# Hybrid encoder layer on one Trainium2 core: weight loads queued apart from their splits, output-weight steps taken singly, SiLU by tanh, and mixer A's queries transposed half a head earlier

## The chip, the cores and the metric

The kernel runs on one core of a Trainium2 chip. The metric is device time in microseconds of one execution. Three runs of the kernel before gave 913.66, 912.55 and 913.62 us, median 913.62.

Names of the profile: PE is TensorE's matmul stream and PEld its weight loads, DVE is VectorE, ACT is ScalarE, POOL is GpSimd, SP is the queue that issues most DMAs. L61 is line 61 of the kernel.

## The reference

One layer of a bidirectional encoder over 512 tokens and 16 meta tokens, width 2048, float32:

```python
hn = rmsnorm(h, pre_norm_g)
proj = hn @ w_in
qa, ka, va, ga, qb, kb, vb, gb = split(proj)
ya = gqa_axial_mixer(qa, ka, va, ...) * silu(ga)
yb = diff_attn_mixer(qb, kb, vb, ...) * silu(gb)
y = concat([ya, yb]) @ w_out
out = (h + rmsnorm(y, post_norm_g))[n_meta:]
```

Mixer A is attention with 8 query heads of 128 over 2 key heads, with an RMS norm and a rotary turn of queries and keys. Mixer B is differential attention: 8 heads, each with two softmaxes over 64-wide halves and a distance penalty, subtracted from each other. Both have a SiLU gate of their width.

## The kernel before, in words

**Splits.** Every float32 operand of a matmul is cut in two parts, high and low, so that three matmuls (high by high, low by high, high by low) give the precision. A weight block of 128 x 1024 is a *chunk*: SP loads it into a buffer `st` (three of them), ACT copies it to `wh` (L156) and DVE subtracts to get `wl` (L157), three buffers each. `fetch` (L206) hands one chunk to the matmuls and keeps two more ready or in preparation. `dense_T` (L212) projects 128 columns of `w_in` from two chunks, with 16 x 3 matmuls of 512 columns for the real tokens (`REAL`), or twice as many of 264 columns for all tokens (`KEYS`).

**Stages, in order.** The start; mixer B, where for each of 8 heads the gate, values, keys and queries are projected while the head before them attends; mixer A's keys, values and two groups of queries (`queries_A`); the eight gates of mixer A; the output product in four quarters (`product`, tiles `po`), built on sums of weight blocks.

**Attention beside the projections.** A recording layer (`Lanes`) keeps a clock of matmul time. An attention task is a generator that records a few matmuls, then yields a lag from the table `LAG`; `dense_T` polls the tasks after every three matmuls. So PE's order is fixed by the lags, and Tile's scheduler orders the other engines around it. A tile of 128 queries makes scores `sc` on PE (one PSUM buffer for all tiles), which DVE takes out together with the row maximum (L521 in mixer B, L624 in mixer A), ACT makes the exponentials (L529, L627), POOL scales them (L534, L629), DVE turns them in 32 x 32 blocks (L448). After two tiles, half a head, the result goes to DRAM and back regrouped (`turn<-pt`, `pl<-turn`), is split (`ph`, `pl`, L337 and L340) and meets the values on PE (`pv`).

**Mixer A's queries.** At a head's start `attention_A` (L597) transposes its queries on PE (`tr<-ident,qn`), splits them on ACT and DVE into `qh` and `qlA`, yields the lag `qA`, and takes four tiles with the lag `scA` between them. Head 4 waits for the second group of queries.

**Output-weight sums.** `weigh` (L805) makes 32 sums of blocks of `w_out` in DRAM, while mixer B runs: SP copies a block (`ws<-in_w_o` or `ws<-ws`), then POOL issues a DMA that adds another block onto it (L809). A call with n=2 takes two steps in a row, and the second of them issues the addition to the block whose copy was issued just before.

**Gates.** `gate` (L423) and `silu_A` (L583) take the projection from PSUM with DVE (times the row scale `rB`), then ACT applies its Silu. Silu, Exp and Sqrt each bring ACT_TABLE_LOADs into ACT's stream.

Of the kernel before, what the change touches and what calls it, by code (L numbers as in the profile page):

```python
# [10 lines left out]
F32 = mybir.dt.float32  # L11
# [3 lines left out]
ALU = mybir.AluOpType  # L15
# [14 lines left out]


LAG = dict(vals=3.5, bank=2.8, bankA=1.5, bankB=2.5, turnA=1.5, turnB=1.5, pvA=5.0, pvB=6.0, scB=3.0,
           pB=22.0, ss=6.0, qA=2.35, scA=5.1, pA=16.0, rope=10.2, head=3.85, fin=1.35, qn=1.4, norm=4.0, valsA=(10.0, 7.0),
           steps=(3.0, 2.5, 2.0, 2.0), stepsK=(2.5, 2.0, 1.5))

AHEAD = -60
# [70 lines left out]
def kernel(ctx: ExitStack, tc: tile.TileContext, xT, xn, xm, w_s, w_t, w_q, w_o,  # L107
# [31 lines left out]
    def load(out, in_):  # L139

        tc.keep_in_program_order(nc.sync.dma_start(out=out, in_=in_))


    def wload(src, n=1024, dma=nc.sync.dma_start, parts=1):
        st = wp.tile([P, 1024], F32, name="st", tag="st")
        ws = None
        for i in range(parts):
            c = slice(i * n // parts, (i + 1) * n // parts)
            dma(out=st[:, c], in_=src if parts == 1 else src[:, c])
            ws = wsplit(st, c, ws)  # L150
        return ws
# [49 lines left out]
        mm(ps, wl, xh[k][:, n0:n1], start=False, stop=(k == KT - 1))  # L201


    todo, chunks = [], []

    def fetch(ahead=2):  # L206
        while todo and len(chunks) <= ahead:
            src = todo.pop(0)
            chunks.append(src() if callable(src) else wload(src))
        return chunks.pop(0)  # L210

    def dense_T(segs, pss=None, half=None):  # L212

        pss = pss or [pd.tile([P, 512], F32, name="pd", tag="pd") for _ in segs]
        for k0 in range(0, KT, 8):
            wh, wl = fetch()
            for k in range(k0, k0 + 8):
                c = slice((k - k0) * P, (k - k0 + 1) * P)
                for (n0, n1), ps in zip(segs, pss):
                    three(ps[:, :n1 - n0], wh[:, c], wl[:, c], k, n0, n1)  # L220
                    lanes.poll()
                if half and k == 8:
                    half()
        return pss
# [117 lines left out]
    def keys_B(pss, after=nullcontext):  # L342
        kf = ap.tile([P, NT], F32, name="kf", tag="tT")
        halves(pss, kf)
        s1 = ap.tile([P, NT], F32R, name="s1", tag="s1")
        s2 = ap.tile([P, NT], F32R, name="s2", tag="s2")
        with after():
            hi(s1[L], kf[L])
            hi(s2[U], kf[U])
            lo(s1[U], kf[L], s1[L])  # L350
            lo(s2[L], kf[U], s2[U])
        return s1, s2
# [43 lines left out]
    def values(pss, lag=LAG["vals"]):  # L396
# [23 lines left out]

        return (vh, vl, vm), lanes.spawn(turn(), lag)

    def gate(pss, name):  # L423
        g = gp.tile([P, SEQ], F32, name=name, tag="g", bufs=4)
        nc.vector.tensor_tensor(out=g, in0=pss[0], in1=rB[:, NM:], op=ALU.mult)
        nc.scalar.activation(g, g, AF.Silu)
        return g


    pv_last, maxima = [None], []  # L430
# [2 lines left out]
    def whole():  # L433

        while pv_open[0]:
            yield 0.1
# [144 lines left out]
        return oA[h] is not None  # L581

    def silu_A(pss):  # L583
        g = gp.tile([P, SEQ], F32, name="gt", tag="gt")
        nc.vector.tensor_tensor(out=g, in0=pss[0], in1=rB[:, NM:], op=ALU.mult)
        nc.scalar.activation(g, g, AF.Silu)
        return g

    def gate_A(h, g):
        nc.vector.tensor_tensor(out=oA[h], in0=oA[h], in1=g, op=ALU.mult)  # L590
# [3 lines left out]
    ASCALE = 1.0 / math.sqrt(P)  # L594
    zed = []

    def attention_A(h, qn, q_task, k, k_task, v, v_task):  # L597
        while h == 4 and not q_task[3]:
            yield 0.3
        qh = ap.tile([P, SEQ], F32R, name="qh", tag="q1")  # L600
        ql = ap.tile([P, SEQ], F32R, name="qlA", tag="q2")
        tr = ptr.tile([P, 512], F32, name="tr", tag="tr")
        for t in range(TT):
            transpose(tr[:, t * P:(t + 1) * P], qn[t][:, h % 4, :], ident)
        hi(dealt(qh), by_token(tr))
        lo(dealt(ql), by_token(tr), dealt(qh))
        yield LAG["qA"]
        while not k_task[3]:
            yield 0.3
        kh, kl = k  # L610
        last = None
        for half in range(2):
            pt = ap.tile([P, 1088], F32, name="pt", tag="pt")
            for t in (2 * half, 2 * half + 1):
                tq = slice(t * P, (t + 1) * P)
                mx = ap.tile([P, 1], F32, name="mxA", tag="mx", bufs=4)
                sm = ap.tile([P, 1], F32, name="smA", tag="sm", bufs=4)
                sc = psc.tile([P, 2, 512], F32, name="sc", tag="sc")
                for i, (n0, n1) in enumerate(KEYS):
                    mm(sc[:, i, :HALF], qh[:, tq], kh[:, n0:n1], start=True, stop=False)  # L620
                    mm(sc[:, i, :HALF], qh[:, tq], kl[:, n0:n1], start=False, stop=False)
                    mm(sc[:, i, :HALF], ql[:, tq], kh[:, n0:n1], start=False, stop=True)
                p = ap.tile([P, NT], F32, name="p", tag="p", bufs=4)
                maxima.append(nc.vector.tensor_tensor_reduce(  # L624
                    out=two(p), in0=sc[:, :, :HALF], in1=two(zed[0][:, :NT]), scale=-ASCALE,
                    scalar=3.0e38, op0=ALU.add, op1=ALU.min, accum_out=mx))
                nc.scalar.activation(p, p, AF.Exp, scale=-1.0, bias=mx, accum_out=sm)  # L627
                nc.vector.reciprocal(out=sm, in_=sm)  # L628
                nc.gpsimd.tensor_scalar(out=p, in0=p, scalar1=sm, scalar2=1.0,  # L629
                                        op0=ALU.mult, op1=ALU.mult)  # L630
                turned(pt, p, t % 2)
                if t % 2 == 0:
                    yield LAG["scA"]
            last = spawn_pv(v_task, p_times_v(regroup(pt), v, lambda pv, half=half:
                            nc.scalar.activation(half_of(oA[h], half), by_quad(pv), AF.Copy), h),
                            LAG["pA"])
            if half == 0:
                yield LAG["scA"]
        over[NH + h] = last
# [162 lines left out]
        steps += [(S[2][i], S[1][i], block(p, 0, 1, i)) for i in range(4)]  # L802
        steps += [(S[3][i], block(p, 0, 0, i), block(p, 1, 0, i)) for i in range(4)]

    def weigh(n=1):  # L805
        for _ in range(n):
            if adds:
                dst, src = adds.pop(0)
                nc.gpsimd.dma_start(out=dst, in_=src, accum_op=ALU.add)  # L809
            if steps:  # L810
                dst, src, add = steps.pop(0)
                load(dst, src)
                adds.append((dst, add))

    def otile(name, n, dt=F32R):
        return xtile(name, n, dt)[:, NM:NT]
# [48 lines left out]
    def finish_head(h):  # L865
        lanes.finish(heads[h])
        lanes.finish(over[h])

    for h in range(NH):
        heads[h] = lanes.spawn(attention_B(h, qs, ks, *v), LAG["head"], heads[h - 1])  # L870
        if h == 2:
            tables()
        if h > 0:
            weigh(2)
            gB[h] = gate(dense_T(REAL), f"gB{h}")
        if h + 1 < NH:
            if h:
                weigh(2)
            pss = dense_T(KEYS)
            if h:  # L880
                finish_head(h - 1)
            v = values(pss)
            if h:
                weigh()
            ks = keys_B(dense_T(KEYS))
            qs = queries_B(h + 1, dense_T(REAL))
    weigh()
    def start_heads(grp, qn, q_task, k, v):
# [13 lines left out]

    start_heads(0, *queries_A(0, zeros), kA, vA)
    second_q = queries_A(1)
    kA = keys_A(dense_T(KEYS))
    start_heads(1, *second_q, kA, values(dense_T(KEYS), LAG["valsA"][1]))
    assert not steps and not adds
# [57 lines left out]
    def product(ops, pss, more=False, beside=None, done=None, ahead=2):  # L965


        def step(u, i, ws):
            for j in range(2):
                bh, bl = ops(i, j, u)  # L970
                c = slice(j * 512, (j + 1) * 512)
                wh, wl = ws[j] if isinstance(ws, list) else [w[:, c] for w in ws]
                mm(pss[u], bh, wh, start=(i + j == 0 and not more), stop=False,
                   skip_group_check=more)
                mm(pss[u], bl, wh, start=False, stop=False, skip_group_check=more)
                mm(pss[u], bh, wl, start=False, stop=(i + j == 4), skip_group_check=more)
                lanes.poll()

        for i in range(1 if done else 4):
            ws = fetch(ahead)  # L980
            for u in range(2):
                step(u, i, ws)
            if beside:
                beside(i)
        if done:
            last = [fetch(len(todo)) for _ in range(3)]
            for u in range(2):
                for i in range(3):
                    step(u, 1 + i, last[i])
                done(u, pss[u])  # L990
        return pss
# [259 lines left out]
```

## Time and profile before

| what | value |
|---|---|
| median of three runs | 913.62 us |
| the profiled execution, its own time | 910.12 us |
| its span, first to last instruction | 908.3 us |
| mean granted TensorE clock | 0.984 |
| ACT busy | 498.6 us (55%) |
| DVE busy | 633.0 us (70%) |
| POOL busy | 126.7 us (14%) |
| ACT_TABLE_LOAD, one | 1283 ns |

Idle time that a row of the timeline puts in brackets is that of the engine before the instruction, with what ended it. A row of a window gives its length, each engine's busy time with its count of instructions, then the granted clock, the DMA engines' busy share, and GB/s.

### The profile page before, as it was taken

To read this page: it belongs to the slowest core of one execution; us is meant where nothing else is said; L and a number is where in the kernel's file an instruction comes from. 1 tells how busy PE (TensorE), PEld (TensorE's weight loads), DVE (VectorE), ACT (ScalarE), POOL (GpSimd) and SP (SyncE) were. 2 spreads that over 40 slices of the span, in tenths; PEclk is the share of its full clock that TensorE was granted. 3 is DMA by queue.
4 is the path that set the end of the run, shared out by engine and by line. 5 is a ranking of instruction groups with operands and counts; after the bars stand their busy time and mean duration, and the time that the engine had idled before them with its cause. 6 is when DMAs were issued, how large, how long until landed. Compare 5 with 4: busy or idle time off the path is not lost. (4 is left out here: it accounts for less than half of the span.)

```text
span 908.3 us, 14068 instructions
## 1 busy us (share of the span) xinstructions
PE 877.6 (97%) x5130; PEld 777.5 (86%) x5130; DVE 633.0 (70%) x1137; ACT 498.6 (55%) x844; POOL 126.7 (14%) x168
## 2 busy tenths in 40 slices
PE   9999999799989999999999999989989899999996
PEld 8999898798979989899898888978878788888884
DVE  6677785576846868575783485788664775876886
ACT  6564664445646456473754444566674565665561
POOL 0101112011111211111020021341211120000010
PEclk9999999899999999999999999999999899999998
DMA  9748759678595785968353334456566568889883
GB/s 342 260 152 238 196 180 264 169 227 218 158 287 131 225 255 157 291 171 254 115 180 93 105 92 153 136 156 180 169 167 187 179 197 306 289 284 305 294 257 150
DMA packets 80677, 185.49 MB, mean 204 GB/s; under 512 B 15136, under 2 KB 38560, under 8 KB 80224
## 3 DMA queue, kind: packets, MB, share of 16 engines
q1 hardware_dynamic: 75856, 167.81, 56.4%
q0 software_dynamic: 4608, 16.78, 10.7%
q8 instruction: 40, 0.66, 0.3%
q14 instruction: 29, 0.24, 0.1%
q10 hardware_dynamic: 144, 0.01, 0.0%
HBM read 158.34 MB, written 59.77 MB: 240 GB/s over the span
## 5 line engine op out<-in xcount | busy, mean ns | idle before, releaser
L61 PE MATMUL pd<-xh,wh 128*128 128x264 f32 (+1 forms) x992 | 328.6, 331 | 0.1
L61 PE MATMUL pd<-xl,wh 128*128 128x264 f32 (+1 forms) x992 | 325.7, 328 | 0.1
L61 PE MATMUL pd<-xh,wl 128*128 128x264 f32 (+1 forms) x992 | 324.6, 327 | 0.0
L156 ACT ACTIVATE wh<-st 128x1024 fp32r<-128x1024 f32 (+2 forms) x159 | 165.4, 1041 | 187.0 <-PE pd L61 95.4
L157 DVE TENSOR_TENSOR wl<-st,wh 128x1024 fp32r<-128x1024 f32 (+2 forms) x159 | 191.1, 1202 | 92.9 <-ACT wh L156 91.3
L61 PEld LDWEIGHTS pd<-xh,wl 128*128 128x128 f32 x992 | 188.3, 190 | 16.3 <-DVE wl L157 0.2
L61 PEld LDWEIGHTS pd<-xh,wh 128*128 128x128 f32 x992 | 188.8, 190 | 12.6 <-ACT wh L156 0.4
L61 PEld LDWEIGHTS pd<-xl,wh 128*128 128x128 f32 x992 | 188.9, 190 | 11.1 <-DVE xl L192 0.4
L529 ACT ACTIVATE p<-p,mx 128x528 f32<-128x528 f32 x64 | 47.1, 736 | 57.0 <-DVE mx L521 56.8
L448 DVE STREAM_TRANSPOSE pt<-p 128x512 f32<-128x512 f32 x64 | 45.2, 706 | 10.7 <-POOL p L629 9.9
L534 POOL TENSOR_SCALAR p<-p,sm 128x528 f32<-128x528 f32 x32 | 23.0, 718 | 208.9 <-DVE sm L531 208.7
L61 PE MATMUL pd<-wh,xh 128*128 128x512 f32 x128 | 50.4, 394 | 0.0
L61 PE MATMUL pd<-wh,xl 128*128 128x512 f32 x128 | 49.9, 390 | 0.0
L61 PE MATMUL pd<-wl,xh 128*128 128x512 f32 x128 | 49.9, 390 | 0.0
L521 DVE CUSTOM_DVE_ANT_0 p<-sc,dist 128x528 f32<-128x528 f32 x64 | 44.0, 688 | 6.5 <-PE sc L61 6.0
L627 ACT ACTIVATE p<-p,mxA 128x528 f32<-128x528 f32 x32 | 23.5, 735 | 40.1 <-DVE mxA L624 40.0
L340 DVE TENSOR_TENSOR pl<-pl,ph 128x1024 fp32r<-128x1024 f32 x32 | 40.4, 1261 | 5.7 <-ACT ph L337 5.2
L61 PE MATMUL sc<-s,q 128*128 128x264 f32 x128 | 35.6, 297 | 8.9 <-DVE mx L521 6.6
L809 POOL DMA_DIRECT2D ws<-in_w_o_dram x32 | 26.6, 841 | 121.9 <-DMA ws<-ws 54.2
L629 POOL TENSOR_SCALAR p<-p,smA 128x528 f32<-128x528 f32 x32 | 25.8, 806 | 122.1 <-DVE smA L628 118.4
L61 PE MATMUL pv<-ph,vh 128*128 128x256 f32 x128 | 37.2, 291 | 2.9 <-DMA st<-in_w_t_dram 2.9
L536 DVE SCALAR_TENSOR_TENSOR p<-p,c 128x528 f32<-128x528 f32 x32 | 24.5, 766 | 21.4 <-POOL p L534 21.2
(223 smaller groups left out, 1578.8 us busy)
## 6 DMA issues: line engine op xcount, KB each, us to landing
st<-in_w_t_dram SPq DMA_DIRECT2D x82, 512.0 KB, 5.5
turn<-pt SPq DMA_DIRECT2D x32, 544.0 KB, 3.0
ws<-in_w_o_dram POOLq DMA_DIRECT2D x32, 512.0 KB, 9.3
pl<-turn SPq DMA_DIRECT2D x128, 128.0 KB, 3.7
st<-ws SPq DMA_DIRECT2D x32, 512.0 KB, 4.5
st<-in_w_o_dram SPq DMA_DIRECT2D x22, 512.0 KB, 4.7
ws<-in_w_o_dram SPq DMA_DIRECT2D x16, 512.0 KB, 7.5
ws<-ws SPq DMA_DIRECT2D x16, 512.0 KB, 6.3
```

What stands on the lines that cost most here:

```text
L61: self._add(self.nc.tensor.matmul(out, lhsT, rhs, start=start, stop=stop, **kw), us)
L156: splits.append((nc.scalar.activation(wh[:, c], st[:, c], AF.Copy), nc.vector.tensor_tensor(out=wl[:, c], in0=st[:, c], in1=wh[:, c].bitca ...
L157: nc.vector.tensor_tensor(out=wl[:, c], in0=st[:, c], in1=wh[:, c].bitcast(F32), op=ALU.subtract)))
L340: nc.vector.tensor_tensor(out=dst, in0=src, in1=h.bitcast(F32), op=ALU.subtract)
L448: nc.vector.transpose(pt[:, :1024].rearrange("p (m c t q) -> p c m t q", m=4, c=TT, t=2)[:, :, :, j], p[:, NM:].rearrange("p (c m q) -> p ...
L521: maxima.append(nc.vector.tensor_tensor_reduce(out=two(p), in0=sc[:, :, :HALF], in1=two(dist[:, w0:w0 + NT]), scale=-0.125 / slope(h), sca ...
L529: nc.scalar.activation(p2[m], p2[m], AF.Exp, scale=-1.0, bias=mx[:, m:m + 1], accum_out=sm[:, m:m + 1])
L534: nc.gpsimd.tensor_scalar(out=p2[0], in0=p2[0], scalar1=sm[:, 0:1], scalar2=1.0, op0=ALU.mult, op1=ALU.mult)
L536: nc.vector.scalar_tensor_tensor(out=p2[0], in0=p2[1], scalar=c2, in1=p2[0], op0=ALU.mult, op1=ALU.add)
L627: nc.scalar.activation(p, p, AF.Exp, scale=-1.0, bias=mx, accum_out=sm)
L629: nc.gpsimd.tensor_scalar(out=p, in0=p, scalar1=sm, scalar2=1.0, op0=ALU.mult, op1=ALU.mult)
L809: nc.gpsimd.dma_start(out=dst, in_=src, accum_op=ALU.add)
```

## The change

Four edits and two numbers. (1) `fetch` keeps a list `landing` of chunks that are loaded and not yet split; it tops the list up to two, so a chunk's load stands in the program up to two chunks ahead of its split. (2) `weigh` takes one step at a time, and adds to a block only when another copy has been issued since; its calls stand at five places of a head. (3) SiLU is written as (tanh(z/2) + 1) z/2: DVE makes z/2, ACT writes tanh into the projection's own PSUM bank, DVE multiplies; the bank is held until then. (4) A head of mixer A transposes and splits the queries of the next head ahead of its own third tile; for head 3 that waits for the second group of queries. The lag `scA` goes from 5.1 to 5.5, `pA` (from a half head's end to its `pv`) from 16 to 13.5.

```diff
-           pB=22.0, ss=6.0, qA=2.35, scA=5.1, pA=16.0, ...
+           pB=22.0, ss=6.0, qA=2.35, scA=5.5, pA=13.5, ...
...
-    todo, chunks = [], []
+    todo, chunks, landing = [], [], []
+    def bring():
+        src = todo.pop(0)
+        if not callable(src):
+            st = wp.tile([P, 1024], F32, name="st", tag="st")
+            nc.sync.dma_start(out=st, in_=src)
+            src = lambda: wsplit(st)
+        landing.append(src)
     def fetch(ahead=2):
-        while todo and len(chunks) <= ahead:
-            src = todo.pop(0)
-            chunks.append(src() if callable(src) else wload(src))
+        while (todo or landing) and len(chunks) <= ahead:
+            if not landing:
+                bring()
+            chunks.append(landing.pop(0)())
+        while todo and len(landing) < 2 and not callable(todo[0]):
+            bring()
         return chunks.pop(0)
...
+    def silu(pss, g):
+        nc.vector.scalar_tensor_tensor(out=g, in0=pss[0], scalar=0.5, in1=rB[:, NM:],
+                                       op0=ALU.mult, op1=ALU.mult)
+        nc.scalar.activation(pss[0], g, AF.Tanh)
+        nc.vector.scalar_tensor_tensor(out=g, in0=pss[0], scalar=1.0, in1=g, op0=ALU.add,
+                                       op1=ALU.mult)
+        return g
...
-        nc.vector.tensor_tensor(out=g, in0=pss[0], in1=rB[:, NM:], op=ALU.mult)
-        nc.scalar.activation(g, g, AF.Silu)
...
+    def part_queries(h, qn):
...
     def attention_A(h, qn, q_task, k, k_task, v, v_task):
         while h == 4 and not q_task[3]:
             yield 0.3
...
-        yield LAG["qA"]
+        if h == 0:
+            part_queries(h, qn)
+            yield LAG["qA"]
+        qh, ql = parts_q[h]
...
+            if half and h + 1 < NH:
+                while h == 3 and not next_q[0][1][3]:
+                    yield 0.3
+                yield from whole()
+                part_queries(h + 1, qn if h != 3 else next_q[0][0])
...
-    def weigh(n=1):
-        for _ in range(n):
-            if adds:
+    def weigh():
+        if len(adds) > (1 if steps else 0):
...
         if h > 0:
-            weigh(2)
-            gB[h] = gate(dense_T(REAL), f"gB{h}")
+            weigh()
+            gB[h] = gate(dense_T(REAL, half=weigh), f"gB{h}")
+            weigh()
         if h + 1 < NH:
-            if h:
-                weigh(2)
             pss = dense_T(KEYS)
             if h:
+                weigh()
                 finish_head(h - 1)
             v = values(pss)
+            ks = keys_B(dense_T(KEYS))
             if h:
                 weigh()
-            ks = keys_B(dense_T(KEYS))
             qs = queries_B(h + 1, dense_T(REAL))
```

PE's order is the same before and after outside mixer A's attention. There, at the passage from head 1 to head 2 (`sc_6167` is head 1's last tile, the `tr` rows are head 2's queries; 24 rows follow the last one shown ahead of head 2's first tile), before:

```order
L61 MATMUL sc_6167<-kl_5009,qh_5914 128x264
L61 MATMUL sc_6167<-kh_5008,qlA_5915 128x264
L61 MATMUL pd_5988<-xh13_128,wh_5928 128x264
L61 MATMUL pd_5988<-xl13_144,wh_5928 128x264
L61 MATMUL pd_5988<-xh13_128,wl_5929 128x264
L64 MATMUL tr_6194<-ident_535,qn_5520 128x128
L64 MATMUL tr_6194<-ident_535,qn_5522 128x128
L64 MATMUL tr_6194<-ident_535,qn_5524 128x128
L64 MATMUL tr_6194<-ident_535,qn_5526 128x128
```

The same passage on PE now (`sc_6199` is head 1's last tile, `sc_6227` head 2's first):

```order
L61 MATMUL sc_6199<-kl_5021,qh_5868 128x264
L61 MATMUL sc_6199<-kh_5020,qlA_5869 128x264
L61 MATMUL pd_6000<-xh13_128,wh_5938 128x264
L61 MATMUL pd_6000<-xl13_144,wh_5938 128x264
L61 MATMUL pd_6000<-xh13_128,wl_5939 128x264
L61 MATMUL sc_6227<-kh_5020,qh_6100 128x264
L61 MATMUL sc_6227<-kl_5021,qh_6100 128x264
L61 MATMUL sc_6227<-kh_5020,qlA_6101 128x264
```

The transposes are gone from here (they stand ahead of head 1's third tile), and the next head's first tile follows three projection matmuls behind the last tile. All seven passages between heads are like this: two with three matmuls of 264 columns between the tiles, as here, five with three of 512 columns.

SP in the gates of mixer A, from a load through the copies of mixer B's outputs (`ob<-oscr`) to the next load, before:

```order
L149 DMA st<-in_w_t_dram 128x1024
L929 DMA ob<-oscr_81 128x2x256
L461 DMA pl<-turn 32x4x256 x4
L462 DMA pt<-turn 32x4x64
L455 DMA turn<-pt 128x1088
L591 DMA oscr_86<-oA_6946 128x512
L929 DMA ob<-oscr_82 128x2x256 x2
L461 DMA pl<-turn 32x4x256 x4
L462 DMA pt<-turn 32x4x64
L455 DMA turn<-pt 128x1088
L929 DMA ob<-oscr_83 128x2x256
L929 DMA ob<-oscr_84 128x2x256 x2
```

The same stretch on SP now, from an `ob` group on:

```order
L959 DMA ob<-oscr_82 128x2x256 x2
L959 DMA ob<-oscr_83 128x2x256
L479 DMA pl<-turn 32x4x256 x4
L480 DMA pt<-turn 32x4x64
L473 DMA turn<-pt 128x1088
L210 DMA st<-in_w_t_dram 128x1024
L606 DMA oscr_85<-oA_6366 128x512
L479 DMA pl<-turn 32x4x256 x4
L480 DMA pt<-turn 32x4x64
L473 DMA turn<-pt 128x1088
L210 DMA st<-in_w_t_dram 128x1024 x2
```

Before, no load follows the one at the top until three rows beyond the last one shown; now loads stand behind each of the two `turn` rows. Up to each of the 32 `turn` rows the number of loads differs by at most 2 between the two orders, and in 22 of the 32 it does not differ.

POOL in mixer B, at the additions to blocks 569 to 573 (`pm` belongs to a `pv`; `p` rows are a head's four tiles), before:

```order
L478 TENSOR_SCALAR pm<-pm 32x256
L809 DMA ws_569<-in_w_o_dram 128x1024
L809 DMA ws_570<-in_w_o_dram 128x1024
L809 DMA ws_571<-in_w_o_dram 128x1024
L809 DMA ws_572<-in_w_o_dram 128x1024
L809 DMA ws_573<-in_w_o_dram 128x1024
L534 TENSOR_SCALAR p<-p,sm 128x528 x4
```

and now:

```order
L838 DMA ws_569<-in_w_o_dram 128x1024
L838 DMA ws_570<-in_w_o_dram 128x1024
L838 DMA ws_571<-in_w_o_dram 128x1024
L552 TENSOR_SCALAR p<-p,sm 128x528
L838 DMA ws_572<-in_w_o_dram 128x1024
L552 TENSOR_SCALAR p<-p,sm 128x528 x3
L838 DMA ws_573<-in_w_o_dram 128x1024
L496 TENSOR_SCALAR pm<-pm 32x256
```

All five stood ahead of a head's four tiles; now one stands behind the first tile and one behind the last. ACT has 46 table loads in the order before and 18 now.

More of the change, by code (lines that the diff above doesn't have):

```diff
@@ L32 @@
 LAG = dict(vals=3.5, bank=2.8, bankA=1.5, bankB=2.5, turnA=1.5, turnB=1.5, pvA=5.0, pvB=6.0, scB=3.0,
-           pB=22.0, ss=6.0, qA=2.35, scA=5.1, pA=16.0, rope=10.2, head=3.85, fin=1.35, qn=1.4, norm=4.0, valsA=(10.0, 7.0),
+           pB=22.0, ss=6.0, qA=2.35, scA=5.5, pA=13.5, rope=10.2, head=3.85, fin=1.35, qn=1.4, norm=4.0, valsA=(10.0, 7.0),
            steps=(3.0, 2.5, 2.0, 2.0), stepsK=(2.5, 2.0, 1.5))
@@ L421, in values @@
         return (vh, vl, vm), lanes.spawn(turn(), lag)
+    def silu(pss, g):
[5 more added lines that the diff above has]
+        return g
     def gate(pss, name):
-        g = gp.tile([P, SEQ], F32, name=name, tag="g", bufs=4)
-        nc.vector.tensor_tensor(out=g, in0=pss[0], in1=rB[:, NM:], op=ALU.mult)
-        nc.scalar.activation(g, g, AF.Silu)
-        return g
+        return silu(pss, gp.tile([P, SEQ], F32, name=name, tag="g", bufs=4))
     pv_last, maxima = [None], []
@@ L583, in silu_A @@
     def silu_A(pss):
[L584 to L587, printed above, removed]
+        return silu(pss, gp.tile([P, SEQ], F32, name="gt", tag="gt"))
     def gate_A(h, g):
@@ L595 @@
     zed = []
-    def attention_A(h, qn, q_task, k, k_task, v, v_task):
-        while h == 4 and not q_task[3]:
-            yield 0.3
+    parts_q, next_q = [None] * NH, []
+    def part_queries(h, qn):
         qh = ap.tile([P, SEQ], F32R, name="qh", tag="q1")
@@ L606, in attention_A @@
         lo(dealt(ql), by_token(tr), dealt(qh))
-        yield LAG["qA"]
+        parts_q[h] = qh, ql
+    def attention_A(h, qn, q_task, k, k_task, v, v_task):
+        while h == 4 and not q_task[3]:
+            yield 0.3
[3 more added lines that the diff above has]
+        qh, ql = parts_q[h]
         while not k_task[3]:
@@ L613, in attention_A @@
             pt = ap.tile([P, 1088], F32, name="pt", tag="pt")
+            if half and h + 1 < NH:
+                while h == 3 and not next_q[0][1][3]:
+                    yield 0.3
+                yield from whole()
+                part_queries(h + 1, qn if h != 3 else next_q[0][0])
             for t in (2 * half, 2 * half + 1):
@@ L803 @@
         steps += [(S[3][i], block(p, 0, 0, i), block(p, 1, 0, i)) for i in range(4)]
-    def weigh(n=1):
-        for _ in range(n):
-            if adds:
[L808 to L813, printed above, removed]
+    def weigh():
+        if len(adds) > (1 if steps else 0):
+            dst, src = adds.pop(0)
+            nc.gpsimd.dma_start(out=dst, in_=src, accum_op=ALU.add)
+        if steps:
+            dst, src, add = steps.pop(0)
+            load(dst, src)
+            adds.append((dst, add))
     def otile(name, n, dt=F32R):
@@ L904 @@
     second_q = queries_A(1)
+    next_q.append(second_q)
     kA = keys_A(dense_T(KEYS))
@@ L985, in product @@
         if done:
-            last = [fetch(len(todo)) for _ in range(3)]
+            last = [fetch(len(todo) + len(landing)) for _ in range(3)]
             for u in range(2):
```

## The prediction

> **What bounds the kernel now.** I read the page first, then the chain of waits and PE's own timeline, then the rows around every place where PE stood still, then the windows for the granted clock.
>
> ```profile
> span 908.3 us, 14068 instructions
> PE 877.6 (97%) x5130; PEld 777.5 (86%) x5130; DVE 633.0 (70%) x1137; ACT 498.6 (55%) x844; POOL 126.7 (14%) x168
> ```
>
> PE is the bound: no other engine is near its span, and the change neither adds nor removes a matmul. So only PE's idle stretches, and the clock after them, can be won or lost. PE's timeline has five places with more than 2 us idle. These are the matmuls that ended them, with the idle time in brackets, and smaller waits right behind:
>
> ```profile
> 172.26 0.59 PE L61 MATMUL sc<-s,q 128*128 128x264 f32 x1 [5.89 <-DVE mx L521]
> ...
> 270.57 0.39 PE L61 MATMUL sc<-s,q 128*128 128x264 f32 x1 [2.21 <-ACT q L337]
> 272.00 0.52 PE L61 MATMUL sc<-s,l 128*128 128x264 f32 x1 [1.04 <-DVE l L340]
> ...
> 611.73 0.39 PE L61 MATMUL sc<-kh,qh 128*128 128x264 f32 x1 [3.08 <-ACT qh L337]
> 612.52 0.39 PE L61 MATMUL sc<-kh,qlA 128*128 128x264 f32 x1 [0.28 <-DVE qlA L340]
> ...
> 680.46 0.39 PE L61 MATMUL sc<-kh,qh 128*128 128x264 f32 x1 [2.12 <-ACT qh L337]
> 681.18 0.39 PE L61 MATMUL sc<-kh,qlA 128*128 128x264 f32 x1 [0.21 <-DVE qlA L340]
> ...
> 708.65 0.39 PE L61 MATMUL pv<-ph,vh 128*128 128x256 f32 x1 [2.92 <-DMA st<-in_w_t_dram]
> 710.10 0.58 PE L61 MATMUL pv<-pl,vh 128*128 128x256 f32 x1 [0.94 <-DVE pl L340]
> ```
>
> Behind each of them the granted clock is at one half for a while; these windows are those stretches, from PE's restart where the clock fell earlier (after each window's length come the engines' busy times, then the clock, the DMA share and GB/s):
>
> ```profile
> 172.26:176.53 4.27, 4.27 (x19) 4.27 (x20) 4.27 (x7) 0.81 (x2) 0.00 (x0) 0.50 0.40 120
> 272.00:275.52 3.52, 3.52 (x10) 2.96 (x11) 3.22 (x5) 0.95 (x3) 1.24 (x2) 0.52 0.97 223
> 613.44:616.85 3.41, 3.41 (x13) 2.93 (x12) 3.38 (x11) 1.89 (x3) 0.90 (x1) 0.50 0.86 259
> 681.70:685.12 3.42, 3.42 (x13) 3.03 (x13) 1.10 (x5) 0.83 (x2) 0.71 (x1) 0.50 0.72 256
> 709.01:715.84 6.83, 5.89 (x21) 5.06 (x20) 5.21 (x8) 2.33 (x4) 1.25 (x1) 0.50 0.69 218
> ```
>
> Half the length of such a window is lost while PE works in it: 2.1, 1.7, 1.7, 1.7 and, over the 5.89 us in which PE was busy, 2.9 us. With the idle time the five places cost 5.89 + 2.1 = 8.0, 2.21 + 1.04 + 1.7 = 4.95, 3.08 + 0.28 + 1.7 = 5.1, 2.12 + 0.21 + 1.7 = 4.0 and 2.92 + 0.94 + 2.9 = 6.8 us: 28.8 us of the 908.3.
>
> **The change part by part.** *Steps taken singly.* The first place comes from POOL:
>
> ```profile
> 167.35 0.81 POOL L809 DMA_DIRECT2D ws<-in_w_o_dram  x1 [8.72 <-DMA ws<-ws]
> ...
> 168.99 0.77 DVE L536 SCALAR_TENSOR_TENSOR p<-p,c 128x528 f32<-128x528 f32 x1 [6.85 <-POOL p L534]
> ```
>
> POOL waited 8.72 us to issue an addition onto a block whose copy was still under way; the scaling of a head's tile stood behind it, DVE waited for that for 6.85 us, the next row maximum behind DVE's wait freed the score buffer late, and PE stood. After the change an addition is issued two steps behind its copy, and two steps are never closer than one gate's projection, 16 x 3 matmuls of 512 columns.
>
> ```profile
> 641.36 0.28 PE L61 MATMUL sc<-kh,qlA 128*128 128x264 f32 x1
> 641.47 0.40 PE L61 MATMUL pd<-xh,wh 128*128 128x512 f32 x1
> 641.71 0.40 PE L61 MATMUL pd<-xl,wh 128*128 128x512 f32 x1
> ...
> ws<-ws SPq DMA_DIRECT2D x16, 512.0 KB, 6.3
> ```
>
> By the distance of starts (641.47 to 641.71, 0.24 us) those 48 matmuls are 11.5 us; a copy lands 6.3 us after its issue in the median. So POOL no longer waits there: −8.0. A copy that lands 5 us late would still not hold it.
>
> *Bursts of DMA and the loads.* The second place:
>
> ```profile
> 257.76 1.14 SPq L149 DMA_DIRECT2D st<-in_w_t_dram  x2
> 258.94 1.42 SPq L141 DMA_DIRECT2D ws<-in_w_o_dram  x2
> ...
> 267.64 1.06 ACT L156 ACTIVATE wh<-st 128x1024 fp32r<-128x1024 f32 x1 [5.00 <-DMA st<-in_w_t_dram]
> ...
> st<-in_w_t_dram SPq DMA_DIRECT2D x82, 512.0 KB, 5.5
> ```
>
> The load issued at 257.76 ended ACT's wait only at 267.64, 9.9 us later against 5.5 in the median, with a pair of copies beside it; ACT's queries `q` stood behind that split. Singly placed copies thin this out, and SP's order now has a load right behind the `turn` row that stood ahead of it, in place of two copies and five rows. The slack gained is a few us against a wait of 5.00 us on ACT. I count −4.95; if the load still comes late, 0.
>
> The fifth place is the same queue in the gates of mixer A:
>
> ```profile
> 694.41 0.34 SPq L455 DMA_DIRECT2D turn<-pt  x1
> ...
> 699.79 0.90 SPq L149 DMA_DIRECT2D st<-in_w_t_dram  x2
> ...
> 706.61 1.04 ACT L156 ACTIVATE wh<-st 128x1024 fp32r<-128x1024 f32 x1
> ```
>
> The load came out at 699.79, behind two `turn` rows and the `ob` copies, and its split ran at 706.61. In SP's new order a load stands behind each `turn`, so this one is issued at about 694.8, 5 us earlier, and one more before that: more than the 2.92 us that PE waited. −6.8; bounds 0 and −6.8. What is late next there is `pl` (0.94 us in the row at 710.10), which ACT and DVE split behind the late chunk; with the chunk early it is early too.
>
> *Queries half a head ahead, and tanh.* Places three and four are `qh`, late on ACT. At the fourth:
>
> ```profile
> 674.60 1.28 ACT L586 ACT_TABLE_LOAD   x1
> ...
> 677.80 1.28 ACT L627 ACT_TABLE_LOAD   x1
> ...
> 679.83 0.58 ACT L337 ACTIVATE qh<-tr 128x512 fp32r<-128x512 f32 x1
> ```
>
> Two table loads of the gate's Silu stood ahead of `qh`; both go, since tanh and the exponentials now follow each other without a load in ACT's order (28 of 46 loads go, 28 x 1.28 = 36 us of ACT, which is 55% busy and off the path elsewhere: 0). And `qh` is due half a head, some 11 us, later than it is made. −4.0. The same edit removes the third wait, −5.1. Tanh's price is DVE's second instruction, of this kind:
>
> ```profile
> L378 DVE SCALAR_TENSOR_TENSOR qf<-pd,rB 128x512 f32<-128x512 f32 x8 | 5.5, 690 | 25.9 <-PE pd L61 25.9
> ```
>
> 16 x 0.69 = 11 us on DVE, one per 11 us of gate projection, in stages where DVE is idle a third of the time: 0, at most 2 us where it delays a row maximum. The projection's bank is kept for about 3 us more; in mixer B it is next written by the keys' projection, after the values' 32 x 3 matmuls of 264 columns (0.11 us each by the starts at 641.36 and 641.47, 10.6 us): hidden.
>
> *What the edit adds.* The lag between a head's last tile and the next head's first is gone: three projection matmuls stand between them, and both use the only score buffer. From the last score matmul's start to the next tile there are 0.11 + 3 x 0.24 = 0.8 us in five of the seven passages and 4 x 0.11 = 0.45 us in two. The buffer is free when DVE has taken the tile:
>
> ```profile
> 641.67 0.71 DVE L624 CUSTOM_DVE_ANT_0 p<-sc,zed 128x528 f32<-128x528 f32 x1 [2.27 <-PE sc L61]
> ...
> L157 DVE TENSOR_TENSOR wl<-st,wh 128x1024 fp32r<-128x1024 f32 (+2 forms) x159 | 191.1, 1202 | 92.9 <-ACT wh L156 91.3
> ...
> 582.01 0.28 PE L61 MATMUL sc<-kh,qlA 128*128 128x264 f32 x1
> 584.39 0.67 DVE L624 CUSTOM_DVE_ANT_0 p<-sc,zed 128x528 f32<-128x528 f32 x1
> ...
> 604.77 0.28 PE L61 MATMUL sc<-kh,qlA 128*128 128x264 f32 x1
> 609.62 0.69 DVE L624 CUSTOM_DVE_ANT_0 p<-sc,zed 128x528 f32<-128x528 f32 x1
> ```
>
> With DVE waiting for it, that is 641.36 to 642.38, 1.0 us: a new wait of 0.2 us at the least. If a chunk's subtraction, 1.2 us, is under way, half of that comes on top on average. I take 0.6 for each of the five, between the two and not at their sum because DVE has air there: 3.0 (bounds 1 and 7). The passages 1 to 2 and 2 to 3 lie where DVE turns the second queries and keys and runs behind: 3.05 us from 582.01 to 585.06, 5.54 from 604.77 to 610.31. The first costs 3.05 − 0.45 = 2.6; PE's wait lets DVE catch up by as much, so the second costs 5.54 − 0.45 − 2.6 = 2.5, and one of them takes a half-clock stretch, 1.7. Together 6.8 (bounds 1 and 12). So the third place is not won but moved, and a little dearer.
>
> [...]
>
> The lag `pA` makes `pv` 2.5 us of recorded time earlier; I count 0, since its operands' splits are recorded earlier by as much, and give it a rival.
>
> *The sum.* −28.8 + 3.0 + 6.8 = −19.0 us. The profiled execution took 910.1 us, span and 1.8 us around it, 3.5 below the median of 913.6; from the median, 913.6 − 19.0 = 894.6, about 894.5 us.
>
> **The rivals.** *The passages decide, and it is slower.* If DVE is as far behind at all seven as at 604.77, each costs 5.5 − 0.7 + 1.7 = 6.5 us, 45 together: 913.6 − 28.8 + 45 = 930. It decides from a mean of 28.8 / 7 = 4.1 us per passage. For it: DVE's order is strict, and a chunk's subtraction can stand ahead of each row maximum. Against it: the wait is that long only in one stretch of some 35 us. 0.10, of which 0.03 lies within 0.2% of no change.
>
> *The loads do not really move.* SP's own waits say so:
>
> ```profile
> SPq L149 <- DVE wl L157: 299.5, 95, 9.5
> ```
>
> In 95 places a load already waited for its buffer to be split, so a longer list can't send it earlier; the order differs in 10 of 32 places only. Then places two and five stay: 894.6 + 4.95 + 6.8 = 906.3. Against it: SP's order does differ at just these two. 0.14.
>
> *The earlier `pv` waits.* In the row at 710.10 a `pv` already waited 0.94 us for its `pl`. If the regrouped data comes from DRAM no earlier than now, `pv` comes 2.5 us earlier to it, and half of the 16 half heads of mixer A pay such a wait, that is 8 x 0.94 = 7.5 us: 902. Against it: one row of 16 shows the wait before, and it has the late chunk ahead of it. 0.12.
>
> **How the numbers follow.** The forecast has 0.64. It and the two middle rivals are faster: 0.64 + 0.14 + 0.12 = 0.90; same 0.03; slower 0.07. A measurement of this kernel can tell about 0.2%, 1.8 us, from no change. Low end: all five places gone and the passages at their lower bounds, 913.6 − 28.8 + 2 = 887, and 2 us for small waits in mixer B that thinner DMA could take along: 885. High end: the loads' rival, 906.3, to 907. Above it lie the slower cases and a part of the sums of two rivals, below it little: 2 in 10 outside.
>
> **What would show it.** Right: no POOL wait of several us for a `ws` copy ahead of `p`; no idle PE near 172, 270, 680 and 708; PE rows `sc<-kh,qh` that wait for DVE's row maximum at seven passages, with the two in the crowded stretch near 2.5 us; 18 table loads. Wrong: loads that still land less than 1 us ahead of their split; `pv` rows that wait for `ph` or `pl`; passages over 4 us; a new wait at head 4's transposes for the second queries' turn, which I take as free because head 3's third tile is held back for it.

## The result, and the profile after

The changed kernel takes 906.2 us in the median of 20 runs (901.9 to 909.3), the kernel before 913.1 us beside it (904.3 to 918.3): a ratio of 0.9939, with a 95% interval from 0.9916 to 0.9962. The ratio leaves out two executions of the kernel before, 918.32 and 918.33, that lie over 1.5% above its fastest. The kernel is faster, by about a third of what was forecast. The profiled execution took 909.26 us, the slowest of its 20, where that of the kernel before, 910.12, lies 3 us below its median; so the two traces differ by 0.8 us of span only. The ledger below is made on these two traces, and is that of the changed kernel's slowest execution.

The page's head after the change:

```profile
span 907.5 us, 14056 instructions
PE 874.7 (96%) x5130; PEld 774.6 (85%) x5130; DVE 643.9 (71%) x1153; ACT 461.9 (51%) x816; POOL 126.8 (14%) x168
```

ACT lost 37 us of work (28 table loads) and DVE gained 11; PE is still the bound, and its own idle time still decides. The five places of the kernel before are gone or smaller, and PE's longest waits now are of these kinds (columns: start, duration, engine, line, operation, and in brackets the idle time ahead and what ended it):

```profile
168.06 0.39 PE L61 MATMUL sc<-s,q 128*128 128x264 f32 x1 [1.88 <-DVE mx L539]
...
318.10 0.39 PE L61 MATMUL sc<-s,l 128*128 128x264 f32 x1 [1.17 <-DVE l L352]
...
580.25 0.36 PE L61 MATMUL sc<-kh,qh 128*128 128x264 f32 x1 [2.36 <-DVE mxA L653]
...
605.67 0.56 PE L61 MATMUL sc<-kh,qh 128*128 128x264 f32 x1 [3.48 <-DVE mxA L653]
...
704.27 0.36 PE L61 MATMUL sc<-kh,qh 128*128 128x264 f32 x1 [1.92 <-DVE mxA L653]
...
728.84 0.39 PE L61 MATMUL pv<-ph,vh 128*128 128x256 f32 x1 [1.67 <-ACT ph L349]
...
730.16 0.38 PE L61 MATMUL pv<-pl,vh 128*128 128x256 f32 x1 [0.82 <-DVE pl L352]
```

The grouped waits say how many of each there are (total, times, longest):

```profile
PE sc L61 <- DVE mxA L653: 10.1, 7, 3.5
...
PE sc L61 <- DVE l L352: 4.7, 4, 1.2
...
PE pv L61 <- DVE pl L352: 2.6, 3, 1.0
```

And the half-clock stretches in which PE works are four after the change, of 3.41 us each; at the clock of 0.50 in their rows each is counted as half its length, 1.7 us:

```profile
168.73:172.14 3.41, 3.41 (x18) 3.41 (x17) 2.87 (x6) 0.39 (x3) 0.00 (x0) 0.50 0.24 97
581.75:585.16 3.41, 3.41 (x18) 3.41 (x17) 2.95 (x9) 0.83 (x2) 1.27 (x2) 0.50 0.48 166
605.64:609.05 3.41, 3.38 (x15) 3.41 (x16) 2.65 (x9) 1.57 (x4) 0.70 (x1) 0.50 0.13 24
704.63:708.04 3.41, 3.41 (x16) 3.12 (x15) 1.97 (x8) 1.18 (x4) 1.20 (x2) 0.50 0.05 18
```

So the ledger: the five places gave back 28.8 us, as recorded. In their stead stand the rest of the first place, 1.88 + 1.7 = 3.6; four waits for DVE's `l` in mixer B, 4.7; the seven passages, 10.1 + 3 x 1.7 = 15.2; and the `pv` waits, 1.67 and the three of `pl`, 4.3. Together 27.8, which leaves 1.0 of gain where the spans show 0.8. The forecast had 9.8 for all of it. Of the first place's 3.6, most belongs to this execution: in the five profiles below whose edits touch mixer A alone, PE waits there 1.2 to 1.3 us, and their mean granted clocks are 0.995 to 0.998, where the changed kernel's is 0.990.

### The profile page after: what moved, and what is told of

Read it like the earlier page. It is cut to its first block, busy times and chain, and to the rows that moved or that the text cites. A ratio compares the mean times of both kernels' runs of the same rounds, so it can differ in the third digit from the quotient of the medians.

```text
span 907.5 us, 14056 instructions
## 1 busy us (share of the span) xinstructions
PE 874.7 (96%) x5130; PEld 774.6 (85%) x5130; DVE 643.9 (71%) x1153; ACT 461.9 (51%) x816; POOL 126.8 (14%) x168
## 3 DMA queue, kind: packets, MB, share of 16 engines
q0 software_dynamic: 4608, 16.78, 11.5%
## 5 line engine op out<-in xcount | busy, mean ns | idle before, releaser
L496 POOL TENSOR_SCALAR pm<-pm 32x256 fp32r<-32x256 f32 x32 | 26.7, 834 | 111.7 <-ACT pm L349 77.2
L61 PE MATMUL pv<-pl,vh 128*128 128x256 f32 x128 | 37.4, 292 | 2.6 <-DVE pl L352 2.6
```

What stands on the lines that cost most here:

```text
L61: self._add(self.nc.tensor.matmul(out, lhsT, rhs, start=start, stop=stop, **kw), us)
L496: nc.gpsimd.tensor_scalar(out=pm[32:64], in0=pm[0:32].bitcast(F32), scalar1=1.0, scalar2=1.0, op0=ALU.mult, op1=ALU.mult)
```

## The experiments

All ratios are to the kernel before, timed beside each kernel; the changed kernel stands at 0.9939. A difference between two such ratios is uncertain by 0.4 to 0.5%, and where it is given in us, it is that share of the kernel before.

**A lag ahead of each head's first tile.** In `attention_A`:

```diff
         if h == 0:
             part_queries(h, qn)
-            yield LAG["qA"]
+        yield LAG["qA"]
```

> The changed kernel with one edit: every head of mixer A, not only the first, waits 2.35 us of PE's own time ahead of its first score tile, so the next head's first tile no longer follows three projection matmuls behind the tile before it. Theory: the score buffer's waits at the seven passages (in the changed kernel's profile 0.2, 2.4, 3.5, 0.2, 0.7, 1.2, 1.9 us idle, and three stretches at half clock of 1.7 us: 15 us together) are a price of their own and go; two of them lie where DVE runs behind, and there a part may come back one tile later. Against the kernel before: 0.978 to 0.985, where the changed kernel stands at 0.994. Rival (DVE's queue is the limit in mixer A, the waits only move to the next tile): 0.992 to 0.996, with as much idle PE between 550 and 710 us as in the changed kernel.

Measured: 899.8 us, ratio 0.9886 [0.9851, 0.9921]. No tile waits for a row maximum at a passage any more, so those waits came from the three matmuls of distance and not from DVE's total work. But the gain is 0.5%, not 0.9 to 1.6%. PE's waits by group:

```profile
PE pv L61 <- DVE pl L352: 5.0, 8, 1.2
...
PE tr L64 <- DVE kn L703: 2.3, 1, 2.3
...
PE pv L61 <- ACT ph L349: 1.4, 3, 0.6
```

`pv` now waits eleven times, 6.4 us in all, and the keys' transposes wait once, 2.3 us, so a part of the passages' 15.2 us only stood in front of these. How large a part stays open: the ratios show 5 us won, the two traces 10.5, and the changed kernel's trace is its slowest execution.

**The lag `pA` at 16 again.** `pA=13.5` becomes `pA=16.0`, nothing else.

> The changed kernel with the lag pA at 16 in place of 13.5, so pv comes 2.5 us of recorded time later again. Theory (the earlier pv waits): the pv waits of the changed kernel's profile (640.23, 728.84, 730.16, 740.54: 0.76 + 1.67 + 0.82 + 1.02 = 4.3 us) go, ratio to the kernel before 0.989 in place of 0.994. Rival (the operand is late whatever the lag is, since its split stands behind a chunk's split on ACT and both come later by the same): no change, 0.994, with pv rows that wait as before.

Measured: 895.3 us, ratio 0.9847 [0.9815, 0.9878]: 0.9% (0.5 to 1.3), about 8 us and twice what the `pv` waits alone came to. One number of the change had cost at least about as much as the change as a whole had won, 0.6% (0.4 to 0.8). The trace shows why it is more than `pv`: the passages got cheaper too. DVE at the passage to head 7, with 13.5:

```profile
701.63 1.22 DVE L352 TENSOR_TENSOR pl<-pl,ph 128x1024 fp32r<-128x1024 f32 x1
702.88 0.50 DVE L352 TENSOR_TENSOR pm<-pt,pm 32x256 fp32r<-32x256 f32 x1
703.41 0.71 DVE L653 CUSTOM_DVE_ANT_0 p<-sc,zed 128x528 f32<-128x528 f32 x1
```

The subtraction of `pl` and `pm` for an early `pv` stands right ahead of the row maximum, whose tile had been complete since 701.66. With 16:

```profile
694.38 1.23 DVE L352 TENSOR_TENSOR pl<-pl,ph 128x1024 fp32r<-128x1024 f32 x1 [0.79 <-ACT ph L349]
695.64 0.50 DVE L352 TENSOR_TENSOR pm<-pt,pm 32x256 fp32r<-32x256 f32 x1
696.64 0.71 DVE L653 CUSTOM_DVE_ANT_0 p<-sc,zed 128x528 f32<-128x528 f32 x1 [0.50 <-PE sc L61]
```

Now both are done before the tile is, and it is DVE that waits. PE's rows at three of the passages, and its waits by group:

```profile
577.16 0.36 PE L61 MATMUL sc<-kh,qh 128*128 128x264 f32 x1 [1.60 <-DVE mxA L653]
...
599.65 0.36 PE L61 MATMUL sc<-kh,qh 128*128 128x264 f32 x1 [2.13 <-DVE mxA L653]
...
697.50 0.36 PE L61 MATMUL sc<-kh,qh 128*128 128x264 f32 x1 [0.20 <-DVE mxA L653]
```

```profile
PE sc L61 <- DVE mxA L653: 6.5, 7, 2.1
```

The seven passages cost 6.5 us without a half-clock stretch, 8.7 less than with 13.5, and `pv` 1.5 us in place of 4.3. With the first place at 1.2 and the four waits for `l` at 4.7, the ledger of this trace is 28.8 − 13.9 = 14.9 us of gain; its span, 893.1, is 15.2 below that of the kernel before.

**The queries' splits ahead of `ph` in mixer B.** The changed kernel's ACT and DVE split `ph` and `pl` of the head before ahead of the next head's queries, the kernel before did it the other way round. An ordering edge turns it back:

```diff
...
-        with tc.issue_after(splits[-1][0].ins):
+        with tc.issue_after(splits[-1][0].ins), tc.issue_after(q_last[0].ins):
             hi(ph, pt)
             hi(pm[0:32], pf)
-        lo(pl, pt, ph)
+        with tc.issue_after(q_last[1].ins):
+            lo(pl, pt, ph)
...
```

`q_last` holds the last split of the queries, and `pB` goes from 22 to 22.8.

> The changed kernel with ACT and DVE made to split the next head's queries in mixer B ahead of ph and pl, as they did in the kernel before; for that the lag pB goes from 22 to 22.8. Theory: the four waits of 1.17 us for DVE's l in heads 4 to 7 of mixer B (263.52, 318.10, 373.76, 428.40) come from the splits' order on ACT and DVE alone and go: 4.7 us, ratio to the kernel before 0.989 in place of 0.994. Rival (they come from the chunk's split that both stand behind, and stay): 0.994, four waits of about 1.2 us.

Measured: 905.67 us, 0.9935 [0.9907, 0.9962], no different from the changed kernel. The four waits do go, so the order made them; but nine waits for row maxima stand in mixer B, where the changed kernel has four:

```profile
PE sc L61 <- DVE mx L542: 3.7, 9, 0.7
```

So this term of the ledger is no price that can be had back by the order. What took the rest of the 4.7 us stays open; the profile's span fell by 2.1 us and the medians show nothing.

**All three.** The edits above together.

> The three edits of the other runs together on the changed kernel: 2.35 us ahead of each head's first tile, pA 16, queries split ahead of ph in mixer B. Theory (the waits are separate prices): 15 + 4.3 + 4.7 = 24 us less than the changed kernel if all go, so between 0.967 and 0.978 of the kernel before. Rival (work that is queued on DVE and ACT keeps PE waiting somewhere): the gains of the three don't add up, 0.985 or above.

Measured: 889.18 us, ratio 0.9780 [0.9747, 0.9812]. The passages' lag alone gives 0.5%, `pA` alone 0.9%, this 1.6%: within the uncertainty they add up. Of the 24 us of the sum, 15 came.

**The loads as before.** `fetch` without the list `landing`:

```diff
...
-            if not landing:
-                bring()
-            chunks.append(landing.pop(0)())
-        while todo and len(landing) < 2 and not callable(todo[0]):
-            bring()
+            src = todo.pop(0)
+            chunks.append(src() if callable(src) else wload(src))
...
```

> The changed kernel with fetch as it was: a weight load stands in SP's order with its own chunk's split again, no list of loads ahead of it. Theory (the loads did move, and that is worth places two and five): loads are issued later again, a stall like those of the kernel before near 270 us (4.95 us) or in the gates of mixer A near 705 us (6.8 us) comes back, ratio to the kernel before 1.000 to 1.007, where the changed kernel stands at 0.994. Rival (the loads do not really move, the buffers' splits set them): 0.992 to 0.996 and no new wait for a load.

Measured: 914.71 us, ratio 1.0046 [1.0019, 1.0073]: the list is worth about 1%. Near 270 us nothing comes back, and the stall in the gates lies one head later than expected. POOL, DVE and PE near the first place, without the list:

```profile
166.20 0.81 POOL L826 DMA_DIRECT2D ws<-in_w_o_dram  x1 [12.57 <-DMA ws<-ws]
```

```profile
167.83 0.77 DVE L542 SCALAR_TENSOR_TENSOR p<-p,c 128x528 f32<-128x528 f32 x1 [3.60 <-POOL p L540]
```

```profile
173.32 0.59 PE L61 MATMUL sc<-s,q 128*128 128x264 f32 x1 [4.86 <-DVE mx L527]
...
734.02 0.58 PE L61 MATMUL pv<-ph,vh 128*128 128x256 f32 x1 [3.33 <-ACT ph L337]
```

The first place is back although the steps are single. POOL's 12.57 us are for a copy that left SP at 156.20, behind a load that had waited for its buffer until 155.75, and that landed at 165.70. The `pv` waits 3.33 us for a `ph` that stands on ACT behind a chunk's split:

```profile
730.04 0.60 ACT L427 ACTIVATE pd<-gt 128x512 f32<-128x512 f32 x1 [4.39 <-DVE gt L425]
...
731.98 1.04 ACT L156 ACTIVATE wh<-st 128x1024 fp32r<-128x1024 f32 x1
732.92 1.04 ACT L337 ACTIVATE ph<-pl 128x1024 fp32r<-128x1024 f32 x1
```

That chunk had landed at 726.45; ACT's order put its split behind tanh, for which ACT waited 4.39 us.

**The steps in pairs as before.** `weigh(2)` at its old places, an addition right behind its copy:

```diff
...
-        if len(adds) > (1 if steps else 0):
-            dst, src = adds.pop(0)
+        for _ in range(n):
+            if adds:
+                dst, src = adds.pop(0)
...
```

> The changed kernel with the output weights' steps issued in pairs as before, an addition right behind its copy. Theory (the additions' wait on POOL made the first place): POOL waits of 4 to 9 us for a ws copy stand ahead of the scaling of p again, PE's stall near 168 us goes from 1.9 us and a stretch at half clock back to some 6 us and two stretches, +4 to +5 us: ratio to the kernel before 0.998 to 1.000. Rival (the copies bunch on SP's queue whatever the program's order is, so single steps bring nothing): 0.994.

Measured: 915.8 us, ratio 1.0055 [1.0023, 1.0088]. The time is above what was expected, but the place is not the one: PE waits 1.69 us at 168.39, no more than with single steps. The profiled execution, 910.1 us, was the fastest of twelve that reach 920.9, so it does not show all of the loss.

**Pairs on the better version.** The same edit on the version with the passages' lag and `pA` 16, which stands below at 0.9783 and is called the better version.

> The version with 2.35 us ahead of each head's first tile and pA 16 (0.978 of the kernel before), with the output weights' steps in pairs again. Theory (single steps are worth some 1%, as their undoing in the changed kernel says, and by places in mixer B that come and go from one execution to the next): 0.986 to 0.992, with a wider spread of times, and idle PE in mixer B behind POOL's wait for a ws copy or behind row maxima. Rival (their undoing cost 1% only beside the changed kernel's other waits): 0.976 to 0.981, as with single steps.

Measured: 897.86 us, ratio 0.9877 [0.9834, 0.9921], 0.9% above the same with single steps, so pairs have a price without the changed kernel's other waits too. One of its places, POOL, DVE and PE in turn:

```profile
383.39 0.85 POOL L838 DMA_DIRECT2D ws<-in_w_o_dram  x1 [7.37 <-DMA ws<-ws]
```

```profile
386.10 0.77 DVE L554 SCALAR_TENSOR_TENSOR p<-p,c 128x528 f32<-128x528 f32 x1 [4.23 <-POOL p L552]
```

```profile
388.48 0.39 PE L61 MATMUL sc<-s,q 128*128 128x264 f32 x1 [1.19 <-DVE mx L539]
```

This is the chain that the prediction read at 168.99, only smaller and in more places.

**Silu again.** Both gates with `AF.Silu` on the scaled projection, as before.

> The changed kernel with the gates' Silu back: 28 more table loads of 1.28 us on ACT, 16 instructions of 0.69 us less on DVE. Theory (queries made half a head ahead already hide the table loads, and DVE is what mixer A waits for): 0.990 to 0.996, no slower than the changed kernel. Rival (the table loads delay ph and the exponentials on ACT, which pv waits for at once): 4 us or more slower than the changed kernel, 0.998 to 1.004.

Measured: 907.06 us, ratio 0.9971 [0.9941, 1.0001]; the interval overlaps that of the changed kernel, so tanh is worth something between nothing and some 0.7%, and neither theory is decided.

**`pA` 13.5 in the kernel before.**

> The kernel before with the lag pA at 13.5 in place of 16 and nothing else. Theory (pv 2.5 us earlier is a price of its own, since its splits come up on ACT and DVE ahead of row maxima and pv meets them late): 6 to 11 us slower than the kernel before, ratio 1.007 to 1.012. Rival (it costs only where the next head's first tile follows at once, by the passages): 0.998 to 1.002.

Measured: 913.44 us, ratio 1.0045 [1.0004, 1.0085], between the two. By these figures the earlier `pv` costs about 4 us without any passage of three matmuls, and 8 where those are; the intervals overlap, so that the passages double the price is not shown by the times.

**Queries and lags as before.** The changed kernel with the old `attention_A`, `scA` 5.1 and `pA` 16; the other parts stay.

> The changed kernel with mixer A's queries and its two lags as they were (queries turned at their own head, scA 5.1, pA 16); the other three parts stay. Theory (this part gives places three and four, 9.1 us, and takes about 15 us at the passages and 4 us at pv, two thirds of it by the lag pA): the kernel becomes 8 to 12 us faster than the changed one, ratio to the kernel before 0.981 to 0.986. Rival (by the sum on record the part is even, 9.1 us against 9.8): 0.992 to 0.996.

Measured: 901.52 us, ratio 0.9907 [0.9880, 0.9934], again between the two. Beside the run with `pA` 16 alone (0.9847) it says that the queries' place, with its `scA`, is worth about 0.6%, and the new `pA` takes 0.9%. Its profile has the third place again:

```profile
602.97 0.39 PE L61 MATMUL sc<-kh,qh 128*128 128x264 f32 x1 [3.07 <-ACT qh L349]
```

The fourth does not come back, here (0.92 us at 670.60, for `qlA`) or in the run with Silu, so by these profiles either edit alone is enough for it.

**The lag and `pA`, without the order in mixer B.**

> The changed kernel with 2.35 us ahead of each head's first tile in mixer A and pA 16; mixer B's splits stay in the changed kernel's order. Theory (the order in mixer B is nearly even, its four waits come back as waits for row maxima): like the run with all three edits, 0.975 to 0.981. Rival (the four waits of 1.17 us are a price of their own): 4.7 us more than that run, 0.983 or above.

Measured: 890.69 us, ratio 0.9783 [0.9753, 0.9813], like all three together. The order of splits in mixer B makes no difference here, and these two edits are all that the better version needs.

**`pA` at 18.5 on top.**

> The same with pA at 18.5. Theory (at 16 the pv waits and the crowding ahead of the passages are gone, more lag has nothing left to win): within 0.3% of the run with 16. Rival (every us of lag takes pl's subtraction further from a row maximum): 3 us or more faster than the run with 16.

Measured: 894.68 us, ratio 0.9846 [0.9816, 0.9876], slower than 16 by 0.6%; neither theory had that. Its profiled execution, 890.65 us, is the fastest of six and shows `pv` waits of 0.5, 1.7 and 0.95 us; what the slower executions add isn't settled.

## Why the prediction was wrong

Right were the bound, the five places, and that four of them would go. The loads moved. In the changed kernel's trace, the load and the split of the chunk that made place two, and of the one behind place five's chunk in the gates:

```profile
243.62 0.33 SPq L210 DMA_DIRECT2D st<-in_w_t_dram  x1
...
683.91 0.38 SPq L210 DMA_DIRECT2D st<-in_w_t_dram  x1
```

```profile
258.01 1.06 ACT L156 ACTIVATE wh<-st 128x1024 fp32r<-128x1024 f32 x1 [1.50 <-PE pd L61]
...
699.39 1.06 ACT L156 ACTIVATE wh<-st 128x1024 fp32r<-128x1024 f32 x1 [1.14 <-PE pd L61]
```

They were issued 14 and 16 us earlier than before, and both splits wait for PE to free a buffer, no longer for a DMA. So the rival by which the loads do not move is dead, although its 906.3 us is what was measured: the number came true by other causes. Which edit did it is shown for the gates alone: without the list, place five's load leaves SP at 699.46, as before (699.79), and with it at 671.82. Place two's load leaves at 249.18 without the list, already 8.6 us earlier than before, and neither that run nor the one with pairs stalls near 270; what took place two away is not settled. Table loads are 18, and no tile waits for `qh`.

**The step that failed** is the sentence on the lag: "I count 0, since its operands' splits are recorded earlier by as much". Recorded order is not time. ACT's split of `ph` stands behind the newest chunk's split, by an ordering edge in the kernel (`issue_after`), and that split waits until PE frees `wh`; an earlier record does not bring it forward by as much. On ACT ahead of the `pv` at 728.84 in the changed kernel:

```profile
725.57 1.06 ACT L156 ACTIVATE wh<-st 128x1024 fp32r<-128x1024 f32 x1 [3.37 <-PE pd L61]
...
727.74 1.04 ACT L349 ACTIVATE ph<-pl 128x1024 fp32r<-128x1024 f32 x1
```

And where it is early, `pl` meets the row maximum. The runs give the number 13.5 a cost of 0.9%, about 8 us, where the sum had 0. The rival of the earlier `pv` waits came near this price with 7.5 us, but put all of it on eight `pv` waits, for data that comes late from DRAM. There were four, 4.3 us, and they were for splits on ACT and DVE: the data for the `ph` above had landed at 714.67. By the two traces the larger part, 8.7 us, lay at the passages.

**The passages** were all seven where they were said to be, and dear in the two that were named (2.36 and 3.48 idle). The term was 9.8 and is 15.2 with `pA` 13.5, but 6.5 with 16: its mean is 2.2 us, below the 4.1 at which the slower rival decides. The mis-sizing is the lag's again, and three half-clock stretches in place of one.

**The first place** was counted at its full 8.0 and gave 4.4 in the changed kernel's trace, and, by the wait alone, about 6.7 in the five that show 1.2 to 1.3 us there. The argument measured two steps in PE's time, 11.5 us, against a copy's 6.3 us. But SP spaces the copies, not PE:

```profile
144.54 1.05 SPq L141 DMA_DIRECT2D ws<-ws  x1
145.69 4.55 SPq L210 DMA_DIRECT2D st<-in_w_t_dram  x2
150.33 2.57 SPq L141 DMA_DIRECT2D ws<-ws  x2
```

The second of the two loads waited on SP until DVE's `wl` freed its buffer, at 149.9, and the two copies behind it left within 1.5 us. POOL met them:

```profile
159.72 0.80 POOL L838 DMA_DIRECT2D ws<-in_w_o_dram  x1 [9.34 <-DMA ws<-ws]
160.92 0.82 POOL L838 DMA_DIRECT2D ws<-in_w_o_dram  x1 [0.40 <-DMA ws<-ws]
161.83 0.70 POOL L552 TENSOR_SCALAR p<-p,sm 128x528 f32<-128x528 f32 x1
```

The copy still held POOL for 9.34 us, but what the wait passes on shrank, and DVE's queue behind it is the rest:

```profile
162.56 0.77 DVE L554 SCALAR_TENSOR_TENSOR p<-p,c 128x528 f32<-128x528 f32 x1 [0.63 <-POOL p L552]
163.25 1.22 DVE L157 TENSOR_TENSOR wl<-st,wh 128x1024 fp32r<-128x1024 f32 x1
...
165.11 0.65 DVE L440 SCALAR_TENSOR_TENSOR gB<-pd,gB 128x512 f32<-128x512 f32 x1
165.68 1.75 DVE L584 RECIPROCAL sq<-sq 128x128 f32<-128x128 f32 x2
167.35 0.64 DVE L539 CUSTOM_DVE_ANT_0 p<-sc,dist 128x528 f32<-128x528 f32 x1
```

DVE waits 0.63 us for POOL in place of 6.85, and then the chunk's subtraction, tanh's second instruction and the reciprocals stand ahead of the row maximum. By the runs it was the list of loads that made the difference: in the three profiles without it (the kernel before, the same with `pA` 13.5, and the changed kernel with single steps) PE waits 5.89, 5.49 and 4.86 us here, and in the eleven with it at most 1.88, with pairs 1.69. Single steps earn their 1% elsewhere, by the profiles in mixer B's smaller waits (eleven for row maxima with pairs, 5.8 us, where the changed kernel has four with 2.6), which the prediction had only as a margin of its low end.

**Not in the sum at all** were the four waits for `l`: the scheduler put two splits in another order in mixer B, where PE's order is the same. The forecast read the order at the places that it spoke of, and this was not one. By the run that turns it back it weighs little.

With 0 for the lag made true, by `pA` at 16, the kernel takes 895.3 us; the forecast was 894.5. That closeness is part luck: the kernel before took 911.0 beside it, and 0.9847 of the 913.6 that the forecast starts from is 899.6. By its ratio the changed kernel is at 908.0, 13.5 us above the forecast; the lag accounts for some 8 of them, and in what is left the waits for `l` and the rest of the first place stand against passages that cost less than was counted.

## What to carry to other kernels

Where order is fixed by a table of lags, a lag that moves one engine's work can be paid on the engines that prepare it: look up what their operand waits for, and what stands next in their queue, before counting it as free. Distance in PE's time did not bound what another queue issues: steps that were counted 11.5 us apart left SP within 1.5 us. And a change of several parts should be undone part by part, since here one number of it cost about as much as all of it together had gained.

## What the runs showed of the hardware

Waits of PE of about the same length were followed by a stretch at half clock in some places and not in others. The four stretches after the change, each 3.41 us long at 0.50, start at 168.73, 581.75, 605.64 and 704.63 us: 121, 7 and 29 times 3.413 us apart. In that trace 1.88 us idle ahead of 168.06 and 1.92 us ahead of 704.27 lay whole within the 3.41 us before a stretch, and behind the 1.67 us ahead of 728.84 there was none. In the version with `pA` 16 the passage at 599.65 had 2.13 us idle and no stretch behind it:

```profile
599.65:603.06 3.41, 3.40 (x20) 3.01 (x21) 3.23 (x13) 2.54 (x10) 1.92 (x3) 1.00 0.02 5
```

The 3.41 us that follow this row are at 1.00 too, and so are the 6.8 us behind the 2.27 us that the keys' transposes wait at 605.58 in the run with the passages' lag alone. How long PE is idle is read from ends of matmuls that the profile models. So 2.1 us of idle time cost 2.1 us here, and at 680.46 in the kernel before, with half of the 3.42 us at 0.50 from 681.70, it is counted as 3.8. The length of a wait alone did not tell which it would be; what does is not shown.

The kernel before went from 904 to 918 us in 20 runs, the changed one from 902 to 909, the better version from 887 to 892 in 5. Waits of some 2 us that cost 1.7 us more in one execution than in another could spread times like that, but no run here separates them from other causes.
